# Two-layer hybrid trunk on one core: Gelu, Q head copies and squares put in a new order, two input steps shifted, four subtractions moved to GpSimd, the last update in three pieces

## The chip, the cores and the metric

The kernel runs on one core of one Trainium2 chip, in one launch. The metric is the device time of one execution in microseconds, the median over the runs shown. TensorE is called PE, VectorE DVE, ScalarE ACT, GpSimd POOL, and SP is the queue that starts most of the DMAs.

## The reference, cut to what matters

256 tokens of width 1024 go through two layers. Every sub-layer is normalized before and after and added to the stream: `h = h + rms(f(rms(h)))`, the FFNs with a factor one half.

```python
# layer 0: FFN, recurrent block, FFN
h += 0.5 * rms(swiglu(rms(h), w_gate, w_up, w_down))          # d_ff = 2816
gx = rms(h) @ rg_w_in; gate, rec = gx[:, :1344], gx[:, 1344:]
rec = rg_lru(causal_conv(rec))                                # sigmoid gates, sqrt, a scan over the tokens
h += rms((gelu(gate) * rec) @ rg_w_out)
h += 0.5 * rms(swiglu(...))
k, v, c = shared_kv(rms(h))       # V, the forget gate and K, once, from the stream after layer 0
# layer 1: FFN, attention over the shared k and v, FFN
h += 0.5 * rms(swiglu(...))
q = rms(h) @ w_q                  # 16 heads of 64
h += rms(softmax(q @ k.T + c[q] - c[k], causal) @ v @ w_o)
h += 0.5 * rms(swiglu(...))
```

## The kernel before, in words

The 256 tokens are two tiles of 128, t = 0 and t = 1, and the stream `h` stays in SBUF. All weights are float32. A block of weights arrives by DMA as `raw`, ACT copies its upper part (`whi`, L204) and DVE subtracts the lower part (`wlo`, L205). The activations are split in the same way, and a product is three matmuls: upper by upper (L212), upper activation by lower weight (L213), lower activation by upper weight (L214). `r` units of the recurrent block use the same three as L219 to L221.

The program is a list of items, each a block of weights with its work for t = 0 and for t = 1 (a slot). `run` lets t = 0 go a few slots ahead of t = 1. The recurrent block and attention have orders written out by hand: `RG_ORDER` names gate units (`0g3` is unit 3 of the gate for t = 0), units `r` of the recurrent part and the small gate products `gw`; `ATT_ORDER` names slots of Q and W_o (a bare `0` or `1`), and logits `L`, transposes `T` and values `V` of the attention. Each engine works through its own instructions in a fixed order. That order is made by a scheduler from the order in which the code issues them, and what is issued under `tc.high_priority()` is moved ahead. `defer(n, f)` puts a step n ticks later; a slot ends with a tick.

When a sub-layer's products for one t are done, `enter` updates the stream: ACT squares the two halves (`junk`, L264) and sums them, POOL makes the reciprocal root (`nv` at L255 and L257, then `rstd` at L259), DVE makes `t` (L327 or L329) and the new `h` (L333). Some ticks later `inputs` transposes `h` on PE (L273), multiplies by the gain (`xg`, DVE, L281), and splits the result: the upper part on ACT (L282) and the lower part on DVE (L287). The buffers `xg`, `t`, `hn` and `rrow` share one pool of two, so a `t` can be written only when the `xg` in its place has been read for the last time. After ffn2 of layer 0 there are two destinations: first the inputs of V and of the forget gate (named `hid` in the trace), then those of the next FFN (named `xall`). After ffn1 of layer 0 `normed_x` takes the squares of the new `h`, and DVE scales it (`hn`, L360) ahead of the transposes (L367).

The other places: `gelu` (L794) turns two accumulated banks of PSUM into `tok` with one instruction, and its bank range spans those between the two. `heads_T` scales a 128x512 piece of Q into `htok` (L1089) and transposes it (L1094). The attention's values are copied to `oh` (ACT, L1274) and `ol` (DVE, L1275). The sqrt of the recurrent part is at L964, the one-column Gelu `warm` behind it at L967; the functions of ACT are held in tables, and `ACT_TABLE_LOAD` changes them.

Of the kernel before, what the change touches and what calls it, by code (L numbers as in the profile page):

```python
# [47 lines left out]
def trunk_kernel(ctx: ExitStack, tc: tile.TileContext, A: dict, out: bass.AP):  # L48
    nc = tc.nc
# [41 lines left out]
    def gtbank():  # L91
        return bank("gt")
# [17 lines left out]
    def defer(n, fn, calm=False):  # L110
        pend.append([n, fn, calm])
# [23 lines left out]
    h = [hall[:, t, :] for t in range(2)]  # L135
# [24 lines left out]
    def gains_T(rows, n, c):  # L160
# [4 lines left out]
    GI = {("ffn1", 0): 0, ("ffn1", 1): 8, ("mix", 0): 16, ("mix", 1): 24,  # L165
          ("ffn2", 0): 32, ("ffn2", 1): 40, "kv": 48}
# [7 lines left out]
    def main_dest(gi, t):  # L174
        return (gi, xhi[:, :, t * P:(t + 1) * P], xlo[:, :, t * P:(t + 1) * P])
# [76 lines left out]
    def rstd_of(ss, n, f=1.0):  # L252

        v = spool.tile([P, 1], F32, tag="nv", name=nm("nv"))
        nc.gpsimd.tensor_scalar(v, ss[:, 0:1], 1.0, D * EPS * f * f, ALU.mult, ALU.add)  # L255
        if n == 2:
            nc.gpsimd.tensor_scalar(v, v, 1.0, ss[:, 1:2], ALU.mult, ALU.add)  # L257
        r = spool.tile([P, 1], F32, tag="rstd", name=nm("rstd"), bufs=8)
        nc.gpsimd.tensor_tensor(r, v, mhalf, ALU.pow)  # L259
        return r  # L260

    def square_sum(src, acc, f=1.0):
        junk = spool.tile([P, D], BF16, tag="junk", name=nm("junk"), bufs=1)
        nc.scalar.activation(junk[:, :src.shape[1]], src, AF.Square, scale=f, accum_out=acc)  # L264
# [11 lines left out]
    def x_upper(tp, dest, n):  # L276

        gi, xh, xl = dest
        xg = hpool.tile([P, 4, P], F32, tag="t1", name=nm("xg"), bufs=2)
        g = gT[:, gi + 4 * n:gi + 4 * n + 4].unsqueeze(2).to_broadcast([P, 4, P])  # L280
        nc.vector.tensor_tensor(xg, tp.rearrange("p (a b) -> p a b", a=4), g, ALU.mult)  # L281
        nc.scalar.activation(xh[:, 4 * n:4 * n + 4, :], xg, AF.Copy)  # L282
        return xg

    def x_lower(xg, dest, n):
        gi, xh, xl = dest
        nc.vector.tensor_tensor(xl[:, 4 * n:4 * n + 4, :], xg, xh[:, 4 * n:4 * n + 4, :].bitcast(F32), ALU.subtract)  # L287

    def to_x(tps, dest):

        with tc.high_priority():
            xg = [x_upper(tps[n], dest, n) for n in range(2)]
            for n in range(2):
                x_lower(xg[n], dest, n)

    rs = [None, None]
    rf = [None, None]
# [13 lines left out]
        rcp["v"] = hpool.tile([P, 512], F32, tag="t1", name=nm("rrow"), bufs=2)[:, :S]  # L311
        nc.scalar.activation(rcp["v"], tp[:, :S], AF.Copy)

    def enter(t, dests, pf, gb, half, last=False, normed=False, first=True):

        f = rf[t][:, 0:1] if half else 1.0 / 32
        r_in = rs[t][:, 0:1] if half else None
        ss = new_ss()
        t1 = []
        urgent = tc.high_priority() if first else ExitStack()  # L320
        urgent.__enter__()
        for n in range(2):
            square_sum(pf[n], ss[:, n:n + 1], f)
        for n in range(2):
            t1.append(hpool.tile([P, 512], F32, tag="t1", name=nm("t1"), bufs=2))
            if half:
                nc.vector.scalar_tensor_tensor(t1[n], pf[n], r_in, gb[:, n * 512:(n + 1) * 512], ALU.mult, ALU.mult)  # L327
            else:
                nc.vector.tensor_tensor(t1[n], pf[n], gb[:, n * 512:(n + 1) * 512], ALU.mult)  # L329
        r = rstd_of(ss, 2, 1.0 / 16 if half else f)  # L330
        for n in range(2):
            hn = h[t][:, n * 512:(n + 1) * 512]
            nc.vector.scalar_tensor_tensor(hn, t1[n], r[:, 0:1], hn, ALU.mult, ALU.add)  # L333
            if last:
                nc.sync.dma_start(out[0, t * P:(t + 1) * P, n * 512:(n + 1) * 512], hn)
        urgent.__exit__(None, None, None)
        if last:
            return

        def inputs():  # L340
            tps = [to_tp(h[t], n) for n in range(2)]
            for dest in dests:
                to_x(tps, dest)
            stat(t)
            if t == 1:
                defer(3, lambda: rstd_rows(trbank() if len(dests) > 1 else sparebank()))

        def norm():
            with tc.high_priority():
                normed_x()  # L350

        def normed_x():
            ss = new_ss()
            for n in range(2):
                square_sum(h[t][:, n * 512:(n + 1) * 512], ss[:, n:n + 1])
            rs[t] = rstd_of(ss, 2)
            hn = []
            for n in range(2):
                hn.append(hpool.tile([P, 512], F32, tag="t1", name=nm("hn"), bufs=2))
                nc.vector.tensor_scalar(hn[n], h[t][:, n * 512:(n + 1) * 512], rs[t][:, 0:1], None, ALU.mult)  # L360

            def go():
                tps = []
                for n in range(2):
                    tp = gtbank()
                    for j in range(4):
                        nc.tensor.transpose(tp[:, j * P:(j + 1) * P], hn[n][:, j * P:(j + 1) * P], ident)  # L367
                    tps.append(tp)
                to_x(tps, dests[0])
            defer(6 if t == 1 else 5, go)  # L370

        if normed:
            norm()
        else:
            defer(4 if t == 1 and len(dests) > 1 else 3, inputs)

    def gain_bcast(src):
        gb = hpool.tile([P, D], F32, tag="gb", name=nm("gb"), bufs=1)
# [403 lines left out]
    def gelu(keys):  # L782

        if "all" not in toks:
            toks["all"] = pools["r"].tile([P, 4, 4 * RT], F32, name="tok")
        tok, n = toks["all"], GCOLS[keys[0][0]][1]
        number = {key: [i for i in range(8) if held.get(i) is gacc[key]][0] for key in keys}
        keys = sorted(keys, key=number.get)
        free = [slots[key] for key in ((0, 0), (0, 1))] if keys[0][0] == 2 else [len(slots) + i for i in range(len(keys))]
        for key, i in zip(keys, sorted(free)):  # L790
            slots[key] = i
            toks[key] = tok[:, i, :]
        (a, c), (b, d) = [(slots[key], number[key]) for key in (keys[0], keys[-1])]
        nc.scalar.activation(tok[:, a:b + 1:max(b - a, 1), :n], pall[:, c:d + 1:max(d - c, 1), :n], AF.Gelu_apprx_tanh)  # L794
# [161 lines left out]
    def batch(g):  # L956

        pairs = [p for p in (2 * g, 2 * g + 1)]
        tps, ys = {}, {}

        def roots():
            for (a, b, w) in parts_of(g):
                v = tt[g][:w, a:b, :]
                nc.scalar.activation(v, v, AF.Sqrt)  # L964
# [68 lines left out]
    for p in range(6):  # L1033
        gw_unit(p)
    n_rg = len(items)
    RG_ORDER = ("0g0 0g1 0g2 0g3 0g4 0g5 0g6 0g7 1g0 1g1 r0 1g2 r1 gw0 1g3 1g4 r2 gw1 1g5 1g6 r3 1g7 gw2 "
                "0g8 0g9 0g10 r4 gw3 r5 1g8 1g9 gw4 1g10 gw5").split()
    OUT_ORDER = [0] * 8 + [1] * 5 + [0] * 3 + [1] * 6

    gbox = {}  # L1040
# [6 lines left out]
    def get_yy(t, k):  # L1047
# [2 lines left out]
        return [v[:w, t, k % 4, :] for v in yy[k // 4]]  # L1050

    row_items(A["rg_w_out"][0], [width(i) for i in range(NRT)], get_yy,
              lambda t, accs: enter(t, [main_dest(GI[("ffn2", 0)], t)], accs, gbox["mix0"], False))
    ahead(n_rg, load_gb("mix0", A["mix_post_g"][0]))
    n_wout = len(items)

# [29 lines left out]
    def heads_T(pool, ps, t, n, scale, dst):  # L1086

        tok = pool.tile([P, 512], F32, tag="htok", name=nm("htok"), bufs=2)
        nc.vector.tensor_scalar(tok, ps, rs[t][:, 0:1], scale, ALU.mult, ALU.mult)  # L1089

        def turn():
            tp = bank("mm")
            for j in range(4):
                nc.tensor.transpose(tp[:, j * P:(j + 1) * P], tok[:, j * P:(j + 1) * P], ident)  # L1094
            nc.scalar.activation(dst[:, 4 * n:4 * n + 4, :].rearrange("p a b -> p (a b)"), tp, AF.Copy)
        defer(2, turn)
# [186 lines left out]
    for n in range(2):  # L1283
        proj_items(A["attn_w_q"][0], n * 512, 512, main_x, post_q(n))
    n_q = len(items)
    row_items(A["attn_w_o"][0], [P] * 8, lambda t, k: (att["oh"][t][:, k, :], att["ol"][t][:, k, :]),
              lambda t, accs: enter(t, [main_dest(GI[("ffn2", 1)], t)], accs, gbox["mix1"], False, first=t == 1), first=1)
    ahead(n_q + 2, load_gb("mix1", A["mix_post_g"][1]))
    n_att = len(items)

# [37 lines left out]
    tps = {}  # L1328
# [160 lines left out]
```

## Time and profile before

| | us |
|---|---|
| median of 3 runs | 984.88 (983.8 to 985.16) |
| the profiled execution | 985.4 |
| its span in the trace | 983.7 |
| PE busy | 970.1 (99%) |
| DVE busy | 666.0 (68%) |
| ACT busy | 556.2 (57%) |
| POOL busy | 52.9 (5%) |
| TensorE clock granted, mean | 0.997 |

A row of a timeline has the start in us from the span's beginning, the duration in us, the engine, the line of the source, the operation, what it writes and reads, and how many like it in a row; in brackets the idle time of the engine before it and what ended that. A row of the windows has the busy time of each engine with its count of instructions, the clock granted to TensorE as a share of full speed, the share of DMA time and GB/s. Of 1.7 us of the execution the trace shows nothing: 985.4 is the time, 983.7 the span.

### The profile page before, as it was taken

Reading aid. Unit: us, or ns where it says so; the run is one execution under the profiler, and the core shown is the slowest. Engines: PE = TensorE matmul, PEld = TensorE weight load, DVE = VectorE, ACT = ScalarE, POOL = GpSimd, SP = SyncE. Lnnn points to the kernel's source line nnn. Section 1 sums busy time; section 2 is a strip of 40 time slices with the busy share of each in tenths; the row PEclk is TensorE's granted clock in tenths of the full one; section 3 lists DMA queues with packets and bytes.
Section 4 is the critical chain, followed back from the end, with each engine's and each line's share of the span. In section 5 each row is a group of like instructions: output and inputs, shape, how many; then the busy total and the mean of one; then the engine's idle time right before and its main releaser. Section 6 shows DMA issues by size and latency. Waiting matters only on the chain.

```text
span 983.7 us, 13946 instructions
## 1 busy us (share of the span) xinstructions
PE 970.1 (99%) x5294; PEld 833.3 (85%) x5294; DVE 666.0 (68%) x829; ACT 556.2 (57%) x733; POOL 52.9 (5%) x111
## 2 busy tenths in 40 slices
PE   9999999999999999999999999999999999999997
PEld 7888888898888888888898888888878788888885
DVE  6878754669997766764696667774478766677542
ACT  6666543559886655443565555553458666555431
POOL 3300000100002000000100000000040000000000
PEclk9999999999999999999999999999999999999999
DMA  8876656565346755555467654555584157556531
GB/s 276 269 263 198 203 183 191 168 182 170 102 121 211 228 199 173 176 193 177 123 216 254 208 178 172 194 204 180 172 299 155 52 180 236 171 192 204 180 110 43
DMA packets 94090, 182.07 MB, mean 185 GB/s; under 512 B 11823, under 2 KB 33415, under 8 KB 93895
## 3 DMA queue, kind: packets, MB, share of 16 engines
q1 hardware_dynamic: 93350, 181.10, 56.4%
q8 instruction: 41, 0.67, 0.3%
q0 software_dynamic: 640, 0.07, 0.1%
q14 instruction: 27, 0.21, 0.1%
q10 hardware_dynamic: 32, 0.01, 0.0%
HBM read 180.09 MB, written 1.06 MB: 184 GB/s over the span
## 4 chain that ended last, share of the span: by engine, by line
PE 95%; DVE 2%; ACT 1%; issue 1%; POOL 1%; POOLq 0%; DVEq 0%; ACTq 0%
PE pall L239 31%; PE pall L247 16%; PE pall L212 13%; PE pall L214 13%; PE pall L213 13%; PE pall L219 1%; PE pall L221 1%; PE pall L220 1%; PE pall L906 1%; PE pall L1229 1%; PE pall L1269 1%; ACT junk L264 1%; PE pall L1255 1%; PE pall L911 0%; PE pall L273 0%
## 5 line engine op out<-in xcount | busy, mean ns | idle before, releaser
L205 DVE TENSOR_TENSOR wlo<-raw,whi 128x1024 fp32r<-128x1024 f32 (+4 forms) x328 | 384.7, 1205 | 215.2 <-ACT whi L204 123.5
L204 ACT ACTIVATE whi<-raw 128x1024 fp32r<-128x1024 f32 (+4 forms) x328 | 339.6, 1043 | 215.1 <-PE pall L214 113.9
L239 PE MATMUL pall<-xall,whi 128*128 128x512 f32 x1280 | 299.7, 390 | 0.4 <-DVE xall L1340 0.4
L239 PEld LDWEIGHTS pall<-xall,whi 128*128 128x128 f32 x1280 | 237.3, 188 | 48.2 <-DVE xall L1340 0.9
L247 PEld LDWEIGHTS pall<-xall,wlo 128*128 128x128 f32 x1280 | 159.6, 191 | 3.8 <-DVE wlo L1348 0.3
L247 PE MATMUL pall<-xall,wlo 128*128 128x256 f32 x1280 | 161.3, 283 | 0.0
L212 PE MATMUL pall<-whi,hid 128*128 128x512 f32 (+2 forms) x400 | 153.0, 382 | 0.0
L214 PE MATMUL pall<-whi,hid 128*128 128x512 f32 (+2 forms) x400 | 152.4, 381 | 0.4 <-DVE hid L287 0.4
L213 PE MATMUL pall<-wlo,hid 128*128 128x512 f32 (+2 forms) x400 | 152.4, 381 | 0.0
L214 PEld LDWEIGHTS pall<-whi,hid 128*128 128x128 f32 x400 | 75.1, 188 | 14.5 <-DVE hid L287 0.7
L212 PEld LDWEIGHTS pall<-whi,hid 128*128 128x128 f32 x400 | 75.1, 188 | 13.6
L213 PEld LDWEIGHTS pall<-wlo,hid 128*128 128x128 f32 x400 | 75.1, 188 | 13.5
L212 PE MATMUL pall<-whi,xall 128*128 128x512 f32 (+2 forms) x144 | 57.3, 398 | 1.6 <-ACT tok L794 1.6
L255 POOL TENSOR_SCALAR nv<-ss 128x1 f32<-128x1 f32 x24 | 9.9, 412 | 901.9 <-ACT junk L264 901.8
L214 PE MATMUL pall<-whi,xall 128*128 128x512 f32 (+2 forms) x144 | 55.5, 386 | 0.0
L213 PE MATMUL pall<-wlo,xall 128*128 128x512 f32 (+2 forms) x144 | 55.4, 385 | 0.0
L523 ACT ACTIVATE sil<-pall 128x1024 f32<-128x1024 f32 (+1 forms) x22 | 20.9, 951 | 54.3 <-PE pall L247 54.3
L523 ACT ACTIVATE prod<-pall 128x1024 f32<-128x1024 f32 (+1 forms) x22 | 20.9, 948 | 42.4 <-PE pall L247 42.4
L639 DVE TENSOR_TENSOR hid<-prod,hid 128x1024 fp32r<-128x1024 f32 (+1 forms) x22 | 24.8, 1128 | 25.3 <-ACT hid L638 25.3
L212 PEld LDWEIGHTS pall<-whi,xall 128*128 128x128 f32 x144 | 27.3, 190 | 8.2 <-ACT tok L794 2.1
L214 PEld LDWEIGHTS pall<-whi,xall 128*128 128x128 f32 x144 | 27.3, 190 | 5.6 <-DVE xall L287 0.3
L213 PEld LDWEIGHTS pall<-wlo,xall 128*128 128x128 f32 x144 | 27.4, 190 | 4.5
(200 smaller groups left out, 952.0 us busy)
## 6 DMA issues: line engine op xcount, KB each, us to landing
raw<-in_ffn_w_down_dram SPq DMA_DIRECT2D x88, 512.0 KB
raw<-in_ffn_w_up_dram SPq DMA_DIRECT2D x80, 512.0 KB
raw<-in_ffn_w_gate_dram SPq DMA_DIRECT2D x78, 512.0 KB
raw<-in_rg_w_in_dram SPq DMA_DIRECT2D x20, 504.0 KB
raw<-in_ffn_w_gate_dram SPq DMA_DIRECT2D x20, 256.0 KB
raw<-in_rg_w_out_dram SPq DMA_DIRECT2D x10, 504.0 KB
raw<-in_ffn_w_up_dram SPq DMA_DIRECT2D x16, 256.0 KB
raw<-in_w_kv_dram SPq DMA_DIRECT2D x8, 512.0 KB
```

What stands on the lines that cost most here:

```text
L204: nc.scalar.activation(hi[:parts, c:c + m], rawv[:, c:c + m], AF.Copy)
L205: nc.vector.tensor_tensor(lo[:parts, c:c + m], rawv[:, c:c + m], hi[:parts, c:c + m].bitcast(F32), ALU.subtract)
L212: nc.tensor.matmul(ps, xh, wh, start=first, stop=False)
L213: nc.tensor.matmul(ps, xh, wl, start=False, stop=False)
L214: nc.tensor.matmul(ps, xl, wh, start=False, stop=last)
L219: nc.tensor.matmul(ps, wh, xh, start=first, stop=False)
L220: nc.tensor.matmul(ps, wh, xl, start=False, stop=False)
L239: nc.tensor.matmul(o[:, b], w, moving(k)[0], start=k == 0, stop=False)
L247: nc.tensor.matmul(oh[:, b], w, moving(k)[1], start=False, stop=k == 7)
L255: nc.gpsimd.tensor_scalar(v, ss[:, 0:1], 1.0, D * EPS * f * f, ALU.mult, ALU.add)
L523: nc.scalar.activation(v, pall[:, b:b + m, S:], AF.Copy)
L639: nc.vector.tensor_tensor(lv, pv, hv.bitcast(F32), ALU.subtract)
```

## The change

Seven edits, the squares and the Gelu among them at several places:

```diff
-    def x_lower(xg, dest, n):
+    def x_lower(xg, dest, n, engine):
...
-    def to_x(tps, dest):
+    def to_x(tps, dest, engine=nc.vector):
...
-    def enter(t, dests, pf, gb, half, last=False, normed=False, first=True):
+    def enter(t, dests, pf, gb, half, last=False, normed=False, first=True, wait=3):
...
-        for n in range(2):
-            hn = h[t][:, n * 512:(n + 1) * 512]
-            nc.vector.scalar_tensor_tensor(hn, t1[n], r[:, 0:1], hn, ALU.mult, ALU.add)
+        for (a, b) in [(0, 512), (512, 768), (768, 1024)] if last and t == 1 else [(0, 512), (512, 1024)]:
+            hn = h[t][:, a:b]
+            nc.vector.scalar_tensor_tensor(hn, t1[a // 512][:, a % 512:a % 512 + b - a], r[:, 0:1], hn, ALU.mult, ALU.add)
             if last:
-                nc.sync.dma_start(out[0, t * P:(t + 1) * P, n * 512:(n + 1) * 512], hn)
+                nc.sync.dma_start(out[0, t * P:(t + 1) * P, a:b], hn)
...
-            for dest in dests:
-                to_x(tps, dest)
+            for i, dest in enumerate(dests):
+                to_x(tps, dest, nc.gpsimd if i else nc.vector)
...
-            for n in range(2):
-                square_sum(h[t][:, n * 512:(n + 1) * 512], ss[:, n:n + 1])
-            rs[t] = rstd_of(ss, 2)
+            square_sum(h[t], ss[:, 0:1])
+            rs[t] = rstd_of(ss, 1)
...
-            defer(4 if t == 1 and len(dests) > 1 else 3, inputs)
+            defer(4 if t == 1 and len(dests) > 1 else wait, inputs)
...
-        nc.scalar.activation(tok[...], pall[...], AF.Gelu_apprx_tanh)
+        with tc.high_priority():
+            nc.scalar.activation(tok[...], pall[...], AF.Gelu_apprx_tanh)
...
-            if g < 2:
+            if g == 1:
                 with tc.high_priority():
                     nc.scalar.activation(warm[:RT], tt[g][:, 0, :1], AF.Gelu_apprx_tanh)
...
-    RG_ORDER = (... "1g5 1g6 r3 1g7 gw2 0g8" ...)
+    RG_ORDER = (... "1g5 1g6 1g7 r3 gw2 0g8" ...)
...
-              lambda t, accs: enter(t, [...], accs, gbox["mix0"], False))                   # W_out
+              lambda t, accs: enter(t, [...], accs, gbox["mix0"], False, wait=4 if t == 1 else 3))
...
-        nc.vector.tensor_scalar(tok, ps, rs[t][:, 0:1], scale, ALU.mult, ALU.mult)            # heads_T
+        with tc.high_priority():
+            nc.vector.tensor_scalar(tok, ps, rs[t][:, 0:1], scale, ALU.mult, ALU.mult)
...
-              lambda t, accs: enter(t, [...], accs, gbox["mix1"], False, first=t == 1), first=1)   # W_o
+              lambda t, accs: enter(t, [...], accs, gbox["mix1"], False, first=t == 1, wait=3 if t == 1 else 5), first=1)
```

The number of matmuls stays, and so do the DMAs but for one more at the end. Three places show how the engines' orders move. (The changed program's lines stand up to three higher or lower than those above.)

ACT in the recurrent block, before. `whi` are weights, the first table load serves the sqrt of `tt`, the second the Gelu of `warm`, and `tok` is the Gelu of the gate's units 0 to 7:

```order
L204 ACTIVATE whi_2355<-raw_2353 128x1008
L204 ACTIVATE whi_2409<-raw_2407 128x672
L964 ACT_TABLE_LOAD
L964 ACTIVATE tt_2099<-tt_2099 126x1024
L204 ACTIVATE whi_2430<-raw_2428 126x1024
L967 ACT_TABLE_LOAD
L967 ACTIVATE warm<-tt_2099 126x1
L858 ACTIVATE xc_2278<-pall,par 126x256 x2
L204 ACTIVATE whi_2458<-raw_2456 126x1024
L204 ACTIVATE whi_2510<-raw_2508 126x1024
L917 ACTIVATE th_2308<-pall,hb 126x256 x2
L794 ACTIVATE tok<-pall 128x1008
```

The same place after:

```order
L204 ACTIVATE whi_2310<-raw_2308 128x1008
L204 ACTIVATE whi_2342<-raw_2340 128x672
L794 ACT_TABLE_LOAD
L794 ACTIVATE tok<-pall 128x1008
L965 ACT_TABLE_LOAD
L965 ACTIVATE tt_2093<-tt_2093 126x1024
L204 ACTIVATE whi_2362<-raw_2360 126x1024
L204 ACTIVATE whi_2401<-raw_2399 126x1024
L204 ACTIVATE whi_2435<-raw_2433 126x1024
L859 ACTIVATE xc_2305<-pall,par 126x256 x2
L918 ACT_TABLE_LOAD
```

The Gelu, with a table load of its own, now stands ahead of the sqrt, and `warm` is gone there. On PE the slot `1g7` (six matmuls) stands ahead of the 48 matmuls of `r3` instead of behind them. `r3` writes bank 2, which lies between the banks 0 and 3 that this Gelu reads, and its first matmul now carries a wait for the Gelu; before, the first matmul of `0g8` (bank 1) carried it.

DVE in Q, before. The `wlo` and `xg` belong to the inputs of t = 1, and the `ISA` begins the attention's softmax:

```order
L205 TENSOR_TENSOR wlo_6442<-raw_6439,whi_6441 128x1024
L281 TENSOR_TENSOR xg_6527<-pall,gT 128x512
L281 TENSOR_TENSOR xg_6530<-pall,gT 128x512
L205 TENSOR_TENSOR wlo_6476<-raw_6473,whi_6475 128x1024
L287 TENSOR_TENSOR xall<-xg_6527,xall 128x4x128
L287 TENSOR_TENSOR xall<-xg_6530,xall 128x4x128
L1089 TENSOR_SCALAR htok_6550<-pall,rstd_6405 128x512
L1242 ISA pe_6589,mx_6587<-pall,nb_6484 128x128
```

And after:

```order
L205 TENSOR_TENSOR wlo_6435<-raw_6432,whi_6434 128x1024
L281 TENSOR_TENSOR xg_6520<-pall,gT 128x512
L281 TENSOR_TENSOR xg_6523<-pall,gT 128x512
L205 TENSOR_TENSOR wlo_6469<-raw_6466,whi_6468 128x1024
L1091 TENSOR_SCALAR htok_6543<-pall,rstd_6398 128x512
L287 TENSOR_TENSOR xall<-xg_6520,xall 128x4x128
L287 TENSOR_TENSOR xall<-xg_6523,xall 128x4x128
L1244 ISA pe_6582,mx_6580<-pall,nb_6477 128x128
```

The head copy `htok` now stands ahead of the two lower parts. The later ones move by one softmax reduction. The third place is the entry of V. DVE before: the end of t = 0's first destination (`hid`), its second (`xg`, `xall`), then the update of t = 1:

```order
L287 TENSOR_TENSOR hid_3079<-xg_4383,hid_3079 128x512
L287 TENSOR_TENSOR hid_3079<-xg_4386,hid_3079 128x512
L281 TENSOR_TENSOR xg_4391<-pall,gT 128x512
L281 TENSOR_TENSOR xg_4394<-pall,gT 128x512
L205 TENSOR_TENSOR wlo_4423<-raw_4420,whi_4422 128x680
L287 TENSOR_TENSOR xall<-xg_4391,xall 128x4x128
L287 TENSOR_TENSOR xall<-xg_4394,xall 128x4x128
L327 SCALAR_TENSOR_TENSOR t_683_4461<-pall,rstd_3007,gb_3365 128x512
L327 SCALAR_TENSOR_TENSOR t_684_4463<-pall,rstd_3007,gb_3365 128x512
L333 SCALAR_TENSOR_TENSOR h<-t_683_4461,rstd_4468,h 128x512
L333 SCALAR_TENSOR_TENSOR h<-t_684_4463,rstd_4468,h 128x512
L205 TENSOR_TENSOR wlo_4435<-raw_4432,whi_4434 128x680
```

DVE after:

```order
L287 TENSOR_TENSOR hid_3072<-xg_4376,hid_3072 128x512
L287 TENSOR_TENSOR hid_3072<-xg_4379,hid_3072 128x512
L281 TENSOR_TENSOR xg_4384<-pall,gT 128x512
L281 TENSOR_TENSOR xg_4387<-pall,gT 128x512
L205 TENSOR_TENSOR wlo_4416<-raw_4413,whi_4415 128x680
L327 SCALAR_TENSOR_TENSOR t_681_4454<-pall,rstd_3008,gb_3358 128x512
L205 TENSOR_TENSOR wlo_4428<-raw_4425,whi_4427 128x680
L205 TENSOR_TENSOR wlo_4434<-raw_4431,whi_4433 128x680
L327 SCALAR_TENSOR_TENSOR t_682_4456<-pall,rstd_3008,gb_3358 128x512
L333 SCALAR_TENSOR_TENSOR h<-t_681_4454,rstd_4461,h 128x512
L333 SCALAR_TENSOR_TENSOR h<-t_682_4456,rstd_4461,h 128x512
L205 TENSOR_TENSOR wlo_4468<-raw_4465,whi_4467 128x680
```

POOL after, where `rf` ends the statistics of t = 0 and the last `rstd` serves the update of t = 1:

```order
L305 TENSOR_SCALAR rf_4399<-rstd_4397 128x1
L287 TENSOR_TENSOR xall<-xg_4384,xall 128x4x128
L255 TENSOR_SCALAR nv_4458<-ss_4449 128x1
L287 TENSOR_TENSOR xall<-xg_4387,xall 128x4x128
L257 TENSOR_SCALAR nv_4458<-nv_4458,ss_4449 128x1
L259 TENSOR_TENSOR rstd_4461<-nv_4458,mhalf 128x1
```

The two subtractions leave DVE, two weight splits come forward between the two `t`, and POOL makes the subtractions between the steps of the reciprocal root. Both `t` now wait for one of these subtractions each, since they take the buffers of the `xg` that POOL reads. Two more follow for t = 1.

Of the other edits, `inputs` of W_out for t = 1 and of W_o for t = 0 come one and two ticks later: the transposes for W_out stand six matmuls later on PE, those for W_o behind the values of pair 12 and two slots. On DVE a weight split of 128x1008 stands ahead of both `hn` of t = 1.

More of the change, by code (lines that the diff above doesn't have):

```diff
@@ L283, in x_upper @@
         return xg
-    def x_lower(xg, dest, n):
+    def x_lower(xg, dest, n, engine):
         gi, xh, xl = dest
-        nc.vector.tensor_tensor(xl[:, 4 * n:4 * n + 4, :], xg, xh[:, 4 * n:4 * n + 4, :].bitcast(F32), ALU.subtract)
-    def to_x(tps, dest):
+        engine.tensor_tensor(xl[:, 4 * n:4 * n + 4, :], xg, xh[:, 4 * n:4 * n + 4, :].bitcast(F32), ALU.subtract)
+    def to_x(tps, dest, engine=nc.vector):
         with tc.high_priority():
@@ L293, in to_x @@
             for n in range(2):
-                x_lower(xg[n], dest, n)
+                x_lower(xg[n], dest, n, engine)
     rs = [None, None]
@@ L793, in gelu @@
         (a, c), (b, d) = [(slots[key], number[key]) for key in (keys[0], keys[-1])]
-        nc.scalar.activation(tok[:, a:b + 1:max(b - a, 1), :n], pall[:, c:d + 1:max(d - c, 1), :n], AF.Gelu_apprx_tanh)
+        with tc.high_priority():
+            nc.scalar.activation(tok[:, a:b + 1:max(b - a, 1), :n], pall[:, c:d + 1:max(d - c, 1), :n],
+                                 AF.Gelu_apprx_tanh)
         for key in keys:
@@ L1035, in trunk_kernel @@
     n_rg = len(items)
-    RG_ORDER = ("0g0 0g1 0g2 0g3 0g4 0g5 0g6 0g7 1g0 1g1 r0 1g2 r1 gw0 1g3 1g4 r2 gw1 1g5 1g6 r3 1g7 gw2 "
+    RG_ORDER = ("0g0 0g1 0g2 0g3 0g4 0g5 0g6 0g7 1g0 1g1 r0 1g2 r1 gw0 1g3 1g4 r2 gw1 1g5 1g6 1g7 r3 gw2 "
                 "0g8 0g9 0g10 r4 gw3 r5 1g8 1g9 gw4 1g10 gw5").split()
@@ L1052, in trunk_kernel @@
     row_items(A["rg_w_out"][0], [width(i) for i in range(NRT)], get_yy,
-              lambda t, accs: enter(t, [main_dest(GI[("ffn2", 0)], t)], accs, gbox["mix0"], False))
+              lambda t, accs: enter(t, [main_dest(GI[("ffn2", 0)], t)], accs, gbox["mix0"], False, wait=4 if t == 1 else 3))
     ahead(n_rg, load_gb("mix0", A["mix_post_g"][0]))
@@ L1286, in trunk_kernel @@
     row_items(A["attn_w_o"][0], [P] * 8, lambda t, k: (att["oh"][t][:, k, :], att["ol"][t][:, k, :]),
-              lambda t, accs: enter(t, [main_dest(GI[("ffn2", 1)], t)], accs, gbox["mix1"], False, first=t == 1), first=1)
+              lambda t, accs: enter(t, [main_dest(GI[("ffn2", 1)], t)], accs, gbox["mix1"], False, first=t == 1,
+                                wait=3 if t == 1 else 5), first=1)
     ahead(n_q + 2, load_gb("mix1", A["mix_post_g"][1]))
```

## The prediction

> **What bounds the kernel now.** The page's first part says it.
>
> ```profile
> PE 970.1 (99%) x5294; PEld 833.3 (85%) x5294; DVE 666.0 (68%) x829; ACT 556.2 (57%) x733; POOL 52.9 (5%) x111
> ```
>
> PE has 13.6 us in 983.7 without a matmul, and the change takes no matmul away. So it can gain only where PE waits, or where its clock is cut. The waits of PE, with total us, times and longest, come next.
>
> ```profile
> PE pall L1094 <- DVE htok L1089: 2.3, 1, 2.3
> PE pall L212 <- ACT tok L794: 1.6, 1, 1.6
> ...
> PE pall L212 <- ACT oh L1274: 0.5, 1, 0.5
> ...
> PE pall L214 <- DVE hid L287: 0.4, 1, 0.4
> PE pall L367 <- DVE hn L360: 0.3, 1, 0.3
> ```
>
> These five single stalls (5.1 us) are what the edits aim at. The windows, with PE's busy time first and the granted clock before the DMA share, show that one stall had a sequel.
>
> ```profile
> 728.00:732.00 4.00, 1.84 (x9) 1.18 (x7) 4.00 (x4) 0.00 (x0) 3.83 (x4) 1.00 0.97 401
> 732.00:736.00 4.00, 3.84 (x14) 3.30 (x14) 0.11 (x1) 0.60 (x1) 2.19 (x2) 0.57 1.03 415
> ```
>
> After the 2.3 us without matmuls the clock was 0.57 for 4 us, which costs up to 0.43 x 4 = 1.7 us.
>
> **Q's head copy.** These rows show the place.
>
> ```profile
> 727.39 2.91 POOL L1199 TENSOR_SCALAR_AFFINE_SELECT nb<-nb 128x2048 f32<-128x2048 f32 x1 [3.88 <-DVE xg L281]
> 728.35 3.10 DVE L287 TENSOR_TENSOR xall<-xg,xall 128x512 fp32r<-128x512 f32 x2
> 730.98 0.88 POOL L259 TENSOR_TENSOR rstd<-nv,mhalf 128x1 f32<-128x1 f32 x1
> 731.37 0.74 DVE L1089 TENSOR_SCALAR htok<-pall,rstd 128x512 f32<-128x512 f32 x1
> 732.16 1.11 PE L1094 MATMUL pall<-ident,htok 128*128 128x128 f32 x4 [2.32 <-DVE htok L1089]
> 735.58 0.61 PE L310 MATMUL pall<-ident,rstd 128*128 128x128 f32 x4
> ```
>
> The two lower parts stood 3.1 us on DVE because POOL's mask held the port until 730.30. The head copy, which reads PSUM, waited behind them. After the change it runs at 728.35 and ends at 729.1, before PE's last matmul ends at 729.84. What is late next is L310, the row of rstd: PE would reach it by 731.5 (four transposes and six matmuls), and POOL's rstd ends at 731.86. Before, L310 began at 735.58. The step is worth 735.6 - 731.9 = -3.7 us, the cut clock included. The lower parts still end by 731.5, and `ISA` needs PE's products from 732. The later head copies had no wait here, so I cost them at nothing.
>
> **The Gelu.** ACT and PE stand so:
>
> ```profile
> 238.84 1.28 ACT L964 ACT_TABLE_LOAD   x1
> 240.14 1.06 ACT L964 ACTIVATE tt<-tt 126x1024 f32<-126x1024 f32 x1
> 247.36 1.01 ACT L794 ACTIVATE tok<-pall 128x1008 f32<-128x1008 f32 x1
> ...
> 242.52 0.40 PE L212 MATMUL pall<-whi,xall 128*128 128x504 f32 x1
> 243.91 1.89 PE L906 MATMUL pall<-xc,gw 126*126 126x256 f32 x8
> 248.43 0.42 PE L212 MATMUL pall<-whi,xall 128*128 128x336 f32 x1 [1.62 <-ACT tok L794]
> ```
>
> The stall of `0g8` goes, 1.62 us. But `1g7`, whose six matmuls took the 1.39 us from 242.52 to 243.91, now begins where `r3` began. `r3`, 48 matmuls of 0.118, ran for 5.64 us up to 242.52, so `1g7` ends at 242.52 - 5.64 + 1.39 = 238.3, and its last matmul's tail at 238.4. The Gelu cannot begin then: ACT still makes the two weight copies that end at 238.84, and its table load follows. It takes the sqrt's place, 240.14 to 241.15, and PE idles from 238.4 to 241.2: 2.75 us. So the stall is not removed but moved, and grows by 1.1 us. Nothing hides it, as PE works in order and every later matmul is queued behind `r3`. What follows on ACT and DVE (the sqrt, `xc`, the second gate products) is about 2.3 us later; `r3` itself, the gate products (243.91 to 246.8) and `0g8` to `0g10` are the cover, and PE needs the `xc` only behind them.
>
> A stall of 2.75 us is longer than the one of 2.3 us that cut the clock; the one of 1.6 us left it whole. I take a cut clock, at 1.5 us, just under the 1.7 above; the ends are 0 and 1.7. Term: +1.1 + 1.5 = +2.6. The page "TensorE: Matmul & The Clock Gate" of the Trainium skill (Part 1) says that the clock is halved after at least one idle window of about 3.4 us. By that rule the clock would stay whole here and the sum be 1.5 lower; the row at 732 disagrees, with a cut after 2.3 us.
>
> For the table load, "ScalarE: Activation LUTs" of the Trainium skill (What ACT_TABLE_LOAD costs) adds about 1.38 us of drain to the load. The rows show none: the load ended at 240.12 and the sqrt began at 240.14. By the page the sum would be 1.4 higher.
>
> **The entry of V.** These are DVE, POOL, ACT and PE.
>
> ```profile
> 488.77 0.86 DVE L205 TENSOR_TENSOR wlo<-raw,whi 128x680 fp32r<-128x680 f32 x1
> 489.55 1.30 DVE L287 TENSOR_TENSOR xall<-xg,xall 128x512 fp32r<-128x512 f32 x2
> 490.76 1.47 DVE L327 SCALAR_TENSOR_TENSOR t<-pall,rstd,gb 128x512 f32<-128x512 f32 x2
> 492.57 1.42 DVE L333 SCALAR_TENSOR_TENSOR h<-t,rstd,h 128x512 f32<-128x512 f32 x2 [0.35 <-POOL rstd L259]
> ...
> 489.67 0.61 POOL L255 TENSOR_SCALAR nv<-ss 128x1 f32<-128x1 f32 x1 [4.19 <-ACT junk L264]
> 491.96 0.57 POOL L259 TENSOR_TENSOR rstd<-nv,mhalf 128x1 f32<-128x1 f32 x1
> ...
> 490.68 0.67 ACT L264 ACTIVATE junk<-pall,rf 128x512 bf16<-128x512 f32 x1
> 493.61 1.09 PE L273 MATMUL pall<-ident,h 128*128 128x128 f32 x8
> 498.17 0.43 PE L214 MATMUL pall<-whi,hid 128*128 128x360 f32 x1 [0.37 <-DVE hid L287]
> ```
>
> PE began the transposes at 493.61, just after the first half of `h` (493.3). So the chain to `h` has no slack, and POOL's subtractions now stand in it twice: both `t` wait for one, and the last `nv` stands behind the second. The trace has no such subtraction on POOL. Below, I take the mask alone, which does 2048 columns in 2.01:
>
> ```profile
> 732.30 2.01 POOL L1199 TENSOR_SCALAR_AFFINE_SELECT nb<-nb 128x2048 f32<-128x2048 f32 x1
> 183.65 2.42 DVE L205 TENSOR_TENSOR wlo<-raw,whi 128x1008 fp32r<-128x1008 f32 x2
> 183.98 0.92 POOL L255 TENSOR_SCALAR nv<-ss 128x1 f32<-128x1 f32 x1 [1.70 <-ACT junk L264]
> 185.61 0.60 POOL L257 TENSOR_SCALAR nv<-nv,ss 128x1 f32<-128x1 f32 x1 [0.70 <-ACT junk L264]
> ```
>
> 512 columns are 0.5 us then. Above: two inputs and a start as long as `rstd`, 2 x 0.5 + 0.57 = 1.6. I take 1.05, the middle. An estimate from the Trainium skill's "GPSIMD Engine Reference" (3.1) is a quarter of its 4497 ns, 1.1 us, and the page speaks against this move: elementwise work stays on DVE.
>
> The rows of `nv` say how the engines share: it ended at 184.90 and at 186.21, just as each of the two splits ended (184.86 and 186.07). At 489.67 it waited for the first lower part likewise, and DVE's `xall` at 728.35 waited for POOL. So an instruction of one that reads two tensors in SBUF waits for the other's. Then: first subtraction 489.63 (end of `wlo`) to 490.7; `t` to 491.45; second subtraction 491.0 to 492.05; the first `wlo` behind it to 492.9; `nv`; the second `wlo` to 493.75, `t` to 494.5; `h` to 495.25. PE is 1.6 us late, and 0.25 more for the second half of `h`. The 0.4 at 498.17 goes. Term: +1.85 - 0.4 = +1.4. With 0.5 us a piece the same walk gives +0.2, with 1.6 it gives +2.3; if the engines do not wait for each other, -0.4. The later pair for t = 1 has weight splits with over 1 us of slack beside it.
>
> **The rest.** The squares:
>
> ```profile
> 199.71 0.89 DVE L360 TENSOR_SCALAR hn<-h,rstd 128x512 f32<-128x512 f32 x2 [1.09 <-POOL rstd L259]
> 200.86 0.60 PE L367 MATMUL pall<-ident,hn 128*128 128x128 f32 x4
> 494.08 1.06 ACT L264 ACTIVATE junk<-h 128x1024 bf16<-128x1024 f32 x1 [1.98 <-DVE h L333]
> ```
>
> For t = 0 one square of 1.06 ends about where the second of two did, and the last `nv` still ends when the second `wlo` does (186.07): the 0.3 us stall stays, 0. For t = 1 the square ends 0.4 us later, and `nv` then meets the split of 1.2 us that was moved ahead of `hn`, so `hn` is about 0.85 later. The first `hn` ended at 200.2, and PE came for it at 200.86, 0.66 later: +0.2 (0 to 0.4).
>
> W_o: these rows show it.
>
> ```profile
> 780.87 0.69 DVE L1248 TENSOR_TENSOR pe<-pe,sm 128x512 f32<-128x512 f32 x1
> 781.48 2.36 DVE L205 TENSOR_TENSOR wlo<-raw,whi 128x1024 fp32r<-128x1024 f32 x2
> 781.79 1.04 PE L1255 MATMUL pall<-ident,pe 128*128 128x128 f32 x8
> 785.91 0.50 PE L212 MATMUL pall<-whi,oh 128*128 128x512 f32 x1 [0.47 <-ACT oh L1274]
> ```
>
> Without the transposes of `h`, PE reaches the eight `pe` transposes 0.9 us earlier, at 780.9. Four of them later (781.35) it waits 0.2 for the second `pe`, which ends at 781.56. `oh` then comes in time, but `ol` stands behind three weight splits on DVE, from 781.48 on 1.18 each, to 785.0; it takes 0.4, and PE wants it at 785.05: 0.3 late. -0.5 + 0.5, so 0 (-0.6 to +0.3). W_out: the transposes of t = 1 come six matmuls (1.4 us) later, and I find no wait that then ends differently. The last update: the third piece of `h` ends where the second half did, with one more DMA beside it. Both 0, 0.2 either way.
>
> Sum: -3.7 + 2.6 + 1.4 + 0.2 = +0.5 us, so 985.9 against the profiled 985.4. That execution is 0.5 above the median; the forecast is 985.4.
>
> **Rivals.** *The clock stays whole* after the Gelu's stall (the 1.6 us stall, which left it whole, speaks for it, the 2.3 us one against): 1.5 less, 983.9. The rule of the Trainium skill's "TensorE: Matmul & The Clock Gate" (Part 1), above, makes the same time. *POOL is harmless and the clock whole*: V -0.4 to +0.2, sum -3.7 + 1.1 - 0.1 + 0.2 = -2.5, 982.4. Against it stand the waits of `nv` at 183.98 and 489.67. *POOL's port decides*: at 1.6 us a piece V costs +2.3, and its stall of 2.8 us is past the 2.3 at which the clock was cut: +1.5 more. Sum -3.7 + 2.6 + 3.8 + 0.2 = +2.9, 987.8. It decides from pieces of about 1.3 us up.
>
> **Numbers.** 0.2% is 2.0 us, about what a measurement of this kernel can tell from no change. Forecast 0.38 (its own range 984.4 to 986.4, from the bounds of squares, W_o and tail), whole clock 0.16, harmless POOL 0.21, port 0.25. The first two lie mostly within 2 us of 984.9; a tenth of the chance goes to each side for their ends (0.05 faster, 0.04 slower). Faster 0.26, same 0.45, slower 0.29. The range takes the harmless case and the port: 982.0 to 988.0.
>
> **What would show it.** Right: no stall at L1094 and a clock of 1.00 there; PE idle for `tok` about 2.75 us ahead of `r3`, then a window at a cut clock; `xall` on POOL near 1 us, and a wait of PE for `h` at the transposes of t = 1. Wrong: a Gelu that ends before 240, subtractions under 0.6 us, or transposes at 493.6 less what was gained before.

## The result and the profile after

| | us, median | ratio to the kernel before | 95% interval |
|---|---|---|---|
| before (10 runs) | 985.02 (981.99 to 985.48) | | |
| changed (10 runs) | 986.59 (985.09 to 988.46) | 1.0025 | 1.0015 to 1.0035 |

The change makes the kernel slower by about 2.5 us (1.5 to 3.5): that is the difference of the means, 984.3 and 986.8, to which the ratio belongs; the medians differ by 1.6. The profiled execution of the changed kernel took 987.44 us (985.4 before), its span 985.7 (983.7). The first part of its page:

```profile
PE 972.2 (99%) x5294; PEld 835.1 (85%) x5294; DVE 665.9 (68%) x826; ACT 557.0 (57%) x728; POOL 58.3 (6%) x113
```

PE still does the same 5294 matmuls but is busy for 2.1 us more: some of them ran at a lower clock. POOL has 5.4 us more. PE's waits after (total us, times, longest):

```profile
PE pall L219 <- ACT tok L794: 2.8, 1, 2.8
PE pall L156 <- DVE idle L144: 1.5, 1, 1.5
PE pall L273 <- DVE h L333: 1.5, 1, 1.5
...
PE pall L907 <- issue: 0.4, 1, 0.4
```

All five stalls that the edits aimed at are gone from the list: `htok`, `tok` at L212, `oh`, `hid`, `hn`. Three new ones stand in their place: `r3` waits 2.8 us for the Gelu, the transposes for V wait 1.5 us for `h`, and a gate product waits 0.4. The timeline of ACT and of PE shows the first:

```profile
237.09 1.69 ACT L204 ACTIVATE whi<-raw 128x1008 fp32r<-128x1008 f32 x2
238.80 1.28 ACT L794 ACT_TABLE_LOAD   x1
240.10 1.01 ACT L794 ACTIVATE tok<-pall 128x1008 f32<-128x1008 f32 x1
...
237.99 0.40 PE L214 MATMUL pall<-whi,xall 128*128 128x504 f32 x1
241.16 0.58 PE L219 MATMUL pall<-xall,whi 128*126 128x256 f32 x1 [2.78 <-ACT tok L794]
249.69 1.89 PE L907 MATMUL pall<-xc,gw 126*126 126x256 f32 x8
```

The Gelu stands where the forecast put it, and `r3` starts when it ends. `r3`, which took 5.64 us before, takes 8.53 from 241.16 to 249.69, since the granted clock (before the DMA share) is low behind the stall:

```profile
240.00:244.00 4.00, 2.84 (x13) 2.84 (x14) 1.70 (x4) 3.96 (x5) 0.00 (x0) 0.57 0.69 211
244.00:248.00 4.00, 4.00 (x23) 4.00 (x23) 4.00 (x7) 0.42 (x1) 0.00 (x0) 0.58 0.12 47
```

At Q the same view shows full windows and a clock of 1.00, where before 1.84 us of 4 were busy and the clock fell to 0.57:

```profile
728.00:732.00 4.00, 4.00 (x24) 3.40 (x23) 3.84 (x5) 2.80 (x4) 1.31 (x2) 1.00 1.09 314
732.00:736.00 4.00, 4.00 (x20) 3.27 (x19) 4.00 (x6) 1.57 (x4) 2.46 (x1) 1.00 1.03 414
```

The entry of V, DVE first and then POOL and PE:

```profile
493.37 0.85 DVE L205 TENSOR_TENSOR wlo<-raw,whi 128x680 fp32r<-128x680 f32 x1
495.42 0.75 DVE L327 SCALAR_TENSOR_TENSOR t<-pall,rstd,gb 128x512 f32<-128x512 f32 x1 [1.20 <-POOL xall L287]
496.08 2.21 DVE L205 TENSOR_TENSOR wlo<-raw,whi 128x680 fp32r<-128x680 f32 x2
498.22 0.74 DVE L327 SCALAR_TENSOR_TENSOR t<-pall,rstd,gb 128x512 f32<-128x512 f32 x1
499.03 1.41 DVE L333 SCALAR_TENSOR_TENSOR h<-t,rstd,h 128x512 f32<-128x512 f32 x2
...
493.60 1.78 POOL L287 TENSOR_TENSOR xall<-xg,xall 128x512 fp32r<-128x512 f32 x1 [3.52 <-ACT xall L282]
495.50 1.30 POOL L287 TENSOR_TENSOR xall<-xg,xall 128x512 fp32r<-128x512 f32 x1
496.78 1.56 POOL L257 TENSOR_SCALAR nv<-nv,ss 128x1 f32<-128x1 f32 x1
...
499.84 1.32 PE L273 MATMUL pall<-ident,h 128*128 128x128 f32 x8 [1.48 <-DVE h L333]
```

The first subtraction overlaps a split and takes 1.78 us, the second 1.30; DVE needed 0.65 for each. The first `t` waits for the first subtraction, and `nv` ends (498.34) as the two splits end (498.29), so `rstd` and `h` are late.

### The profile page after: what moved, and what is told of

Same layout as the page of the kernel before. It is cut to its first block, busy times and chain, and to the rows that moved or that the text cites. A ratio compares the mean times of both kernels' runs of the same rounds, so it can differ in the third digit from the quotient of the medians.

```text
span 985.7 us, 13943 instructions
## 1 busy us (share of the span) xinstructions
PE 972.2 (99%) x5294; PEld 835.1 (85%) x5294; DVE 665.9 (68%) x826; ACT 557.0 (57%) x728; POOL 58.3 (6%) x113
## 4 chain that ended last, share of the span: by engine, by line
PE 93%; ACT 2%; DVE 2%; issue 1%; POOL 1%; POOLq 0%; DVEq 0%; ACTq 0%
PE pall L239 31%; PE pall L247 16%; PE pall L212 13%; PE pall L214 13%; PE pall L213 13%; PE pall L219 1%; PE pall L221 1%; PE pall L220 1%; PE pall L907 1%; PE pall L273 1%; PE pall L1231 1%; PE pall L1271 1%; ACT th L918 0%; PE pall L1257 0%; DVE wlo L205 0%
## 5 line engine op out<-in xcount | busy, mean ns | idle before, releaser
L212 PE MATMUL pall<-whi,hid 128*128 128x512 f32 (+2 forms) x400 | 153.0, 382 | 0.0
L214 PE MATMUL pall<-whi,hid 128*128 128x512 f32 (+2 forms) x400 | 152.3, 381 | 0.0
L214 PEld LDWEIGHTS pall<-whi,hid 128*128 128x128 f32 x400 | 75.1, 188 | 13.9
L212 PEld LDWEIGHTS pall<-whi,hid 128*128 128x128 f32 x400 | 75.1, 188 | 13.5
L212 PE MATMUL pall<-whi,xall 128*128 128x512 f32 (+2 forms) x144 | 56.7, 394 | 0.0
L214 PE MATMUL pall<-whi,xall 128*128 128x512 f32 (+2 forms) x144 | 55.2, 383 | 0.0
L212 PEld LDWEIGHTS pall<-whi,xall 128*128 128x128 f32 x144 | 27.1, 188 | 6.5 <-issue 1.9
L214 PEld LDWEIGHTS pall<-whi,xall 128*128 128x128 f32 x144 | 27.1, 188 | 5.5 <-DVE xall L287 0.3
```

Source lines behind the costliest of these rows:

```text
L212: nc.tensor.matmul(ps, xh, wh, start=first, stop=False)
L214: nc.tensor.matmul(ps, xl, wh, start=False, stop=last)
```

## The experiments

The theory: the Gelu edit and V's subtractions cost 4.6 and 1.4 us, Q's head copy gives back 3.9, and the rest does nothing. The rivals: the cut clock is chance and no cost of the edit; the wait for `h` is lateness brought along from the Gelu; the stall at Q was gone anyway. Each ratio is to the kernel before.

**Each part undone alone.** The Gelu's edit:

```diff
-        with tc.high_priority():
-            nc.scalar.activation(tok[...], ..., AF.Gelu_apprx_tanh)
+        nc.scalar.activation(tok[...], ..., AF.Gelu_apprx_tanh)
-            if g == 1:                                   # warm
+            if g < 2:
-    RG_ORDER = "... 1g6 1g7 r3 gw2 ..."
+    RG_ORDER = "... 1g6 r3 1g7 gw2 ..."
```

> The changed kernel (986.6 us) with the Gelu edit alone undone. Theory: that edit costs the 4.1 us by which the trace after is behind at 0g8 (1.15 of stall, 2.9 of clock cut to a half behind it), and 0.5 at 276.6 where gate products meet late xc: 982.0 us, stall of 1.6 us at 0g8 back and clock 1.00 there. Rival, the cut clock is no steady cost of this edit (the profiled run had the lowest clock of ten): only the 1.15 of stall comes back, 985.4. Second rival, the 0.5 at 276.6 has another cause: it stays.

Measured: 982.9 us, ratio 0.9986 (0.9977 to 0.9995). The edit costs 0.0039, 3.8 us; the rival with 1.15 falls. The stall of 1.6 is back at `0g8`, and the wait of 0.4 at the gate product is gone, so the second rival falls too.

V's subtractions:

```diff
-                to_x(tps, dest, nc.gpsimd if i else nc.vector)
+                to_x(tps, dest)
```

> The changed kernel with the second set of lower parts back on DVE. Theory: POOL's pieces of 1.3 to 1.8 us delay both t and the root, PE's wait of 1.5 us for h goes and 0.3 comes back: -1.4, 985.2 us. Rival, the wait comes from the two weight splits that now stand between the two t, not from POOL: order goes back too, so the time is the same 985.2, and a kernel with POOL for t = 1 only has to tell. Second rival, lateness brought from the Gelu, not POOL, makes PE wait: 986.6.

Measured: 985.1 us, 1.0010 (0.9999 to 1.0020): 0.0015, 1.5 us, as the theory had it, though the intervals overlap. The trace decides against the second rival: with the same stall at the Gelu ahead of it, PE no longer waits for `h`, and 0.3 us for `hid` is back; and with the Gelu's edit undone PE still waits 1.5 us for `h`. The first rival gives the same time here; the rows of V above show both at work, since the first `t` waits for POOL and `nv` for the splits.

Q's head copies:

```diff
-        with tc.high_priority():
-            nc.vector.tensor_scalar(tok, ps, rs[t][:, 0:1], scale, ALU.mult, ALU.mult)
+        nc.vector.tensor_scalar(tok, ps, rs[t][:, 0:1], scale, ALU.mult, ALU.mult)
```

> The changed kernel with the head copies in the old place. Theory: the stall of 2.3 us ahead of L1094 returns, and so does the cut clock behind it: +3.9, 990.5 us. Rival, the stall returns but the clock's cut was one execution's: +2.3, 988.9. Second rival, the earlier W_o and V delays have moved POOL's mask away from the lower parts: 0 to +1.

Measured: 988.47 us, 1.0048 (1.0030 to 1.0067), 2.3 us more than the changed kernel. This is the first rival's number, but with an error of 2.1 us the time alone does not exclude the theory's 3.9. The seven runs lie at 986.64 to 987.29 (three), 988.47 (one) and 990.05 to 990.16 (three); the mean granted clock is 0.994 or 0.995 in the last three and 0.997 or 0.998 in the others, so the clock is cut in some executions more than in others. In the profiled one the stall of 2.3 us is back while the clock stays whole:

```profile
732.00:736.00 4.00, 1.68 (x9) 1.06 (x8) 3.85 (x4) 0.00 (x0) 3.74 (x4) 1.00 0.97 395
736.00:740.00 4.00, 4.00 (x33) 3.42 (x34) 0.37 (x3) 1.01 (x3) 2.02 (x1) 1.00 1.01 396
```

The squares, the two shifted inputs and the last update, all as before:

```diff
+            for n in range(2):                                                # normed_x
+                square_sum(h[t][:, n * 512:(n + 1) * 512], ss[:, n:n + 1])
-            square_sum(h[t], ss[:, 0:1])
...
-              ... False, wait=4 if t == 1 else 3))                            # W_out
+              ... False))
-              ... wait=3 if t == 1 else 5), first=1)                          # W_o
+              ... wait=3), first=1)
```

> The changed kernel with the squares, the two shifted inputs and the last update as before. Theory: together nothing: 986.6 us within 0.5, with 0.5 of wait for oh back at W_o and 0.3 for hn back, and some loss at the eight pe transposes gone. Rival, the shifted inputs cost what the trace shows between 783 and 788 (matmuls at half clock, 1.0 us): 985.6.

Measured: 987.38 us, 1.0034 (1.0023 to 1.0045). So these edits gain 0.9 us if anything; the intervals overlap, and the rival, by which they cost 1.0, has no support; the changed kernel's windows from 780 to 788 show a clock of 1.00, not the half clock that it names. Both small stalls return:

```profile
PE pall L212 <- ACT oh L1277: 0.5, 1, 0.5
...
PE pall L367 <- DVE hn L360: 0.3, 1, 0.3
```

**The clock behind the stall.** The gap is filled with matmuls whose results are not used:

```diff
+        if (1, 1) in keys:
+            ps = gtbank()
+            for _ in range(21):
+                nc.tensor.matmul(ps[:, :256], xhi[:, 0, :P], xhi[:, 0, :], start=True, stop=True)
```

> The changed kernel, with 21 matmuls of 256 columns (2.5 us, into a bank that the gate products overwrite) put on PE ahead of r3, where it waits for the Gelu; their results are not used. Theory: the cut clock comes of PE's idleness, its size is chance (half the clock for about 5.9, 3.4, 3.4 and 0 us in four profiled executions with this same stall, so 2.9, 1.6, 1.6 and 0 us lost, 1.5 on average): clock 1.00 there, time 1.5 less, 985.1 us (984.3 to 985.7), and the runs lie closer together. Rival, the cut has to do with what follows (r3's loads) and not with the gap: cut stays, 986.6 or a little more.

Measured: 984.9 us, 1.0015 (1.0005 to 1.0025), 12 runs within 984.4 and 985.8, where the changed kernel's ten spread over 3.4 us. `r3` still starts when the Gelu ends, and the clock is whole:

```profile
242.23 0.38 PE L219 MATMUL pall<-xall,whi 128*126 128x256 f32 x1 [0.29 <-ACT tok L794]
247.98 1.89 PE L911 MATMUL pall<-xc,gw 126*126 126x256 f32 x8
...
240.00:244.00 4.00, 3.71 (x32) 3.51 (x31) 2.28 (x4) 3.96 (x4) 0.00 (x0) 1.00 0.41 139
244.00:248.00 4.00, 4.00 (x37) 4.00 (x36) 3.42 (x6) 2.56 (x3) 0.00 (x0) 1.00 0.44 127
```

One profile with a whole clock would prove little, as one of five without the filling has it too; but all 12 runs have a mean granted clock of 0.998 or 0.999, and the changed kernel's ten have 0.994 to 0.999. So idle time of PE brings the cut. The medians differ by 1.7 us, the ratios by 0.0010, which is 1.0 us with an error of 1.4.

**Why `r3` waits.** One Gelu instruction for each bank:

```diff
-            nc.scalar.activation(tok[:, a:b + 1:max(b - a, 1), :n], pall[:, c:d + 1:max(d - c, 1), :n], AF.Gelu_apprx_tanh)
+            for key, i in zip(keys, sorted(free)):
+                nc.scalar.activation(tok[:, i, :n], pall[:, number[key], :n], AF.Gelu_apprx_tanh)
```

> The changed kernel with the Gelu made by one instruction per bank. Theory: r3 waits only because the one instruction reads banks 0 to 3 as a range and r3 writes bank 2; with two instructions PE does not wait: 2.8 of stall and 1.5 of clock go, a table load more on ACT (the first Gelu moves forward) costs up to 0.5: 982.6 us (982 to 983.5). Rival, ACT is the bound there (two weight copies, the Gelu, a table load more ahead of r3's xc and the gate products): a new wait of 1 to 2.5 us at the gate products, 984 to 985.

Measured: 982.66 us, 0.9988 (0.9979 to 0.9997). PE waits for no `tok`; at the gate products it waits 1.0 us instead of 0.4. Nothing that `r3` needs was missing: it waited since its bank 2 lies between the banks 0 and 3 of one instruction.

**Which of POOL's pairs costs.**

```diff
-                to_x(tps, dest, nc.gpsimd if i else nc.vector)
+                to_x(tps, dest, nc.gpsimd if i and t == 1 else nc.vector)
```

> The changed kernel with POOL's lower parts for t = 1 alone; those of t = 0 are on DVE again. Theory: the cost is all in the first pair, which stands in the chain to h; the second has slack: as without POOL, ratio 1.001 to before (985.1 us on the scale of the changed kernel's 986.6). Rival, both pairs cost through the shared port with the weight splits: half of the 1.5 stays, 985.8.

Measured: 985.2 us, 1.0012 (1.0002 to 1.0021), no wait for `h`. The first pair carries the cost, as the theory had it; half of it in the second pair (1.0018) isn't excluded by the interval. This kernel does not tell POOL's pieces from the two splits that came forward with them, for here both splits stand behind `h` again. In the changed kernel the second pair (on POOL from 505.16 to 507.71) held up two small DVE steps of the forget gate, which took 0.18 us each before, without a wait of PE:

```profile
505.42 1.07 DVE L717 TENSOR_TENSOR l<-az,l 128x16 f32<-128x16 f32 x1
506.52 1.22 DVE L718 TENSOR_TENSOR l<-l 128x16 f32<-128x16 f32 x1
```

**Towards a faster version.** Three kernels in search of one. The first has one Gelu instruction for each bank, the old order of units, the old `warm`, no priority, and V's subtractions on DVE:

> The changed kernel with the Gelu's order and V's lower parts as before, and the Gelu by one instruction per bank: Q's head copies, squares, shifted inputs, last update stay new. Theory: without the Gelu edit the ratio to before is 0.9986, V gives back 1.5 us and the stall of 1.6 us at 0g8 goes: 0.9986 - 0.0015 - 0.0016 = 0.9955. Rival, ACT's table loads (three more) make a new wait in the recurrent block that eats the 1.6: 0.997.

Measured: 984.59 us, 1.0003 (0.9993 to 1.0013): the theory falls, and the rival's 0.997 was too kind. Three table loads come with only the sqrt and one tanh between them, and the last gate product starts 0.1 us after the first tanh behind them (the view names no releaser for it). PE waits 2.6 us, and the clock behind it is 0.56 and 0.59 in the windows from 272 to 280:

```profile
268.24 1.06 ACT L964 ACTIVATE tt<-tt 126x1024 f32<-126x1024 f32 x1
269.32 1.28 ACT L917 ACT_TABLE_LOAD   x1
270.61 0.47 ACT L917 ACTIVATE th<-pall,hb 126x256 f32<-126x256 f32 x1
271.10 1.28 ACT L967 ACT_TABLE_LOAD   x1
272.40 0.20 ACT L967 ACTIVATE warm<-tt 126x1 f32<-126x1 f32 x1
272.51 1.19 ACT L917 ACTIVATE th<-pall,hb 126x256 f32<-126x256 f32 x3
...
273.06 1.97 PE L906 MATMUL pall<-xc,gw 84*84 84x256 f32 x4 [2.56 <-issue]
```

The second keeps one instruction and the new order, moves a bank, and has V's subtractions on DVE:

```diff
+                if (g, t) == (1, 1):
+                    order["mm"].sort(key=lambda b: b != 1)
                 gacc[(g, t)] = mmbank()
```

> The changed kernel with V's lower parts on DVE again and the gate's second accumulator in bank 1 instead of 3, so that the one Gelu reads banks 0 and 1, r2 goes to 3 and r3's bank 2 lies outside. Theory: no wait ahead of r3 as in the kernel with two Gelus (ratio 0.9988), without its extra table load and with a shorter wait at the gate products (0.4 instead of 1.0 us), and V gives 0.0014: 0.9970 (0.9962 to 0.9978). Rival, the table load ahead of the Gelu on ACT makes sqrt, xc and the gate products so late that PE waits there instead: 0.9985.

Measured: 985.5 us, 1.0010 (0.9998 to 1.0021). No wait for `tok`, but the same three loads with the sqrt and a tanh between them, and a wait of 3.1 us at L909 with a clock of 0.59 and 0.55 behind it. The rival was the right mechanism, and larger than its number. The third has the old order and the moved bank:

> As the kernel before in the Gelu's order, with the gate's second accumulator in bank 1; Q's head copies, squares, shifted inputs and last update new, V's lower parts on DVE. Theory: 0.9986 without the Gelu edit, 0.0014 for V, and the 1.6 us of stall ahead of 0g8 go because 0g8's bank now lies outside the Gelu's range: 0.9956, no wait of PE for tok. Rival, what is late next takes the gain: PE reaches the gate products 1.6 us earlier and waits there for ACT: 0.9965 to 0.9972.

Measured: 980.44 us (979.91 to 980.65), 0.9956 (0.9943 to 0.9968). The theory's number, and faster than both kernels. The waits listed for PE are

```profile
PE pall L156 <- DVE idle L144: 1.5, 1, 1.5
PE pall L1096 <- DVE htok L1091: 0.8, 1, 0.8
PE pall L214 <- DVE hid L287: 0.4, 1, 0.4
```

**Q alone.** The kernel before with the head copies' edit only:

> The kernel before with the head copies' new place alone. Theory: 2.3 us of stall go in each execution, and a cut clock in those that have it (1.7 us in the profile of before, none in that of the changed kernel with the old place): -2.3 to -4.0, ratio 0.9968 (0.9959 to 0.9977). Rival, what is late next (the row of the root, L310) eats part: above 0.998.

Measured: 982.15 us, 0.9979 (0.9967 to 0.9990), 2.1 us. It lies between theory and rival, and what eats part isn't L310. A weight split ahead of the head copy is now what POOL's mask holds up:

```profile
727.42 2.01 POOL L1200 TENSOR_SCALAR_AFFINE_SELECT nb<-nb 128x2048 f32<-128x2048 f32 x1 [3.46 <-DMA nb<-ckd]
...
727.66 2.85 DVE L205 TENSOR_TENSOR wlo<-raw,whi 128x1024 fp32r<-128x1024 f32 x1
730.43 0.74 DVE L1090 TENSOR_SCALAR htok<-pall,rstd 128x512 f32<-128x512 f32 x1
...
731.23 0.66 PE L1095 MATMUL pall<-ident,htok 128*128 128x128 f32 x4 [0.92 <-DVE htok L1090]
```

## Why the prediction held, and where its terms were off

The forecast was 985.4 with 982.0 to 988.0; 986.59 lies inside. Its sum said no measurable change, +0.5 us; the measurement says +2.5, and slower by 2 us or more had been given 0.29. That the time lies inside is owed to the width of the range, which reached out to the port rival: the Gelu and Q missed the same way, by 1.2 and 1.4 us. By the undone parts, worked out from the differences of the ratios (their errors are 1.3 to 2.1 us):

| part | predicted | measured |
|---|---|---|
| Gelu | +2.6 | +3.8 |
| entry of V | +1.4 | +1.5 |
| Q's head copy | -3.7 | -2.3 |
| the rest | +0.2 | -0.9 |
| sum | +0.5 | +2.1 |

**Gelu.** The stall was foreseen to a few hundredths (2.75, measured 2.78, from 240.14, measured 240.10), and so was its cause. The clock was taken at 1.5 us, with ends 0 and 1.7. Five profiled executions with this same stall of 2.78 show what that number is. From the first matmul of `r3` to the gate product it is 8.53 us in the changed kernel, 7.26 with V on DVE (241.53 to 248.79), 7.28 with the rest undone (241.32 to 248.60), 7.25 with POOL for t = 1 (241.65 to 248.90), and here, with the head copy undone:

```profile
241.57 0.39 PE L219 MATMUL pall<-xall,whi 128*126 128x256 f32 x1 [2.78 <-ACT tok L794]
247.30 1.89 PE L907 MATMUL pall<-xc,gw 126*126 126x256 f32 x8
```

5.73, which is the time at a whole clock. So the loss is 2.8, 1.5, 1.5, 1.5 and 0 us: its mean is the 1.5 taken, its upper end was too low. That the two agree is luck: the 1.5 was the size of one cut, "just under the 1.7 above", and not a mean over executions with and without one. The Trainium skill's "TensorE: Matmul & The Clock Gate" (Part 1) says that the window which decides is free-running, and that how much of a kernel runs cold varies from run to run; these five agree with the second. Its rule that a whole idle window of about 3.4 us is needed doesn't hold here: 2.78 us cut the clock in four of five. The rival of a whole clock was thus right in one execution, not in the mean.

The term missed 0.5 us. The Gelu's priority applies to its last call too, which I did not cost: it now stands ahead of three of four `th`, and the last gate product starts 0.1 us after the second of the four, with a wait of 0.36; it starts 2.74 us after the gate product ahead of it (273.86), and with the edit undone 2.21 us (269.79 to 272.00) and with no wait. So the rows suggest, though no kernel had that priority alone taken away. These rows are ACT after, then ACT with the edit undone, then PE after:

```profile
275.03 0.46 ACT L918 ACTIVATE th<-pall,hb 126x256 f32<-126x256 f32 x1
275.40 0.74 ACT L794 ACTIVATE tok<-pall 128x672 f32<-128x672 f32 x1
276.03 1.20 ACT L918 ACTIVATE th<-pall,hb 126x256 f32<-126x256 f32 x3
...
270.95 1.55 ACT L916 ACTIVATE th<-pall,hb 126x256 f32<-126x256 f32 x4
272.38 0.74 ACT L793 ACTIVATE tok<-pall 128x672 f32<-128x672 f32 x1
...
276.60 1.34 PE L907 MATMUL pall<-xc,gw 84*84 84x256 f32 x4 [0.36 <-issue]
```

With 1.15, 1.5 and 0.5 the term would have been 3.15; the other 0.65 lies within the error.

**Entry of V.** The size came out for the reasons given. POOL's pieces were longer than the 1.05 taken (1.30 and 1.78), but the first began beside the split and not behind it, so its end came as foreseen. `nv` did meet the splits (1.56 us). The port rival, which asked for pieces from 1.3 us up, had the pieces but not the stall: 1.5 us instead of 2.8, with no cut clock behind it. The Trainium skill's "SBUF — State Buffer" (SBUF: two separate sides) says that a DVE instruction with two SBUF inputs and a GpSimd one that reads SBUF share a port, which the first holds to its end; the 1.78 beside a split against 1.30, and the `nv` of 1.56 that ends with the splits, agree. The waits refute the rival of a harmless POOL; the 1.5 us of time alone, with an error of 1.4, would barely do so.

**Q's head copy.** This term was mis-sized, and it moved the sum most: -3.7 counted the cut clock of one profile as present in every execution. The stall of 2.3 us goes; the cut goes only where it was. Of the 84 runs of the kernel before that were measured beside the experiments, 34 have a mean granted clock of 0.996 or 0.997 and take 984.7 to 986.0 us; the other 50 have 0.998 or 0.999 and take 981.7 to 985.5. The profile of before, with 0.997, is one of the first kind, and the one cut that its windows show ahead of its last matmuls is at Q. The step on what is late next (L310 at 731.9) holds in the changed kernel, where PE does not wait at Q. It fails when the edit stands alone, where 0.9 us of wait for `htok` is left, and with POOL for t = 1 alone and in the fastest kernel, where 0.8 is: there the head copy itself is late, not L310.

**The rest.** The wait of 0.3 for `hn` was said to stay and went: with one square the root needs one `nv` step less behind the splits. At W_o the walk held. The 0.5 for `oh` went, but the eight `pe` transposes take 1.36 us instead of 1.04, and `ol` comes late behind three splits: its weight load waits 0.44 us, and L214 begins at 787.72, 0.18 later than the 0.23 us from one of these matmuls to the next would have it. The list of PE's waits does not show this.

```profile
783.28 1.36 PE L1257 MATMUL pall<-ident,pe 128*128 128x128 f32 x8
787.72 0.19 PEld L214 LDWEIGHTS pall<-whi,ol 128*128 128x128 f32 x1 [0.44 <-DVE ol L1277]
```

All this is too small for the times.

## What to carry to other kernels

Before moving an instruction to end a wait, ask what the wait is for: here one instruction read two accumulators through a range that covered a third, and giving the second accumulator the neighbouring bank, in the old order, ended a stall that reordering only moved. In the new order the moved bank ended that stall too, but another of 3.1 us took its place. A cut clock read from one profile is one draw: weigh it by its mean over executions, on the side where it is gained as on the side where it is lost. A priority set in a helper holds for all its calls; look at each of them.

## What the runs showed of the hardware

The same stall of 2.78 us was followed by a clock cut that lost between 0 and 2.8 us, and a stall of 2.3 us by a cut in one profile and by none in another; the stalls of 2.6 and 3.1 us were followed by one in the one profile that there is of each. Stalls of 1.5 to 1.6 us were not followed by one in these profiles. What decides it in an execution was not tried.
